# A mixture-of-experts decoder layer on one core: more result buffers, expert blocks added without an order among themselves, two small tables moved, and the last norm on VectorE alone

## The chip, the cores and the metric

The kernel runs on one core of one Trainium2 chip. The metric is the time of one execution in microseconds (us), as the device counts it. Five engines work beside each other, each through its own instructions in its own order: TensorE (PE: matrix products; PEld is its loading of weights), VectorE (DVE), ScalarE (ACT), GpSimd (POOL) and SyncE (SP, which here only issues DMA transfers). An engine that meets an instruction whose input is not there waits, and everything behind it on that engine waits with it.

## The reference

A decoder layer on 1024 tokens of width 1024 in float32: a mixer (gated linear attention and a diagonal state-space model side by side), then a feed-forward part with 32 experts, of which every token uses four, each part between RMS norms and with a modulation from a vector c. The change touches the expert part and the last norm. Cut to them:

```python
logits = (xt @ router_w + router_b)
top_val, top_idx = lax.top_k(logits, TOP_K)         # 4 experts of 32 for each token
gate = jax.nn.softmax(top_val, axis=-1)
...
def expert_block(args):                             # a block of up to 128 tokens of one expert
    xblk, e = args
    gu = xblk @ w_gu[e] + b_gu[e]                   # 1024 -> 2 x 1024
    g, up = gu[:, :D_FF], gu[:, D_FF:]
    g = jnp.minimum(g, SWIGLU_LIMIT)
    up = jnp.clip(up, -SWIGLU_LIMIT, SWIGLU_LIMIT)
    act = (up + 1.0) * (g * jax.nn.sigmoid(SWIGLU_ALPHA * g))
    return act @ w_down[e] + b_down[e]              # 1024 -> 1024
...
out = zeros.at[tok_buf].add(yb * w_buf[:, None])    # every token sums its four weighted results
...
h = h + g2 * rmsnorm(ff, ffn_post_g)                # the last norm
```

## The kernel before

**Stages.** The mixer, the router and the sorting of the tokens by expert take the first 600 us or so. Then comes the expert phase, from about 613 to 1959 us, and behind it a short tail with the last norm. The 32 experts stand in eight groups of four. Each group has a gate-and-up phase (32 chunks of weights) and a down phase (16 chunks); a chunk is 512 x 512 float32 weights, 1 MB, and there are 384.

**A chunk.** SP loads it into one of six stages. ACT makes its float16 high part (L1585), DVE the float16 rest, the low part (L1588, one `scalar_tensor_tensor` of 128 x 2048 with a sum into a column of `gacc` that tells overflow at the end). PE multiplies the high part with both halves of the tokens (L1791, L1792) and the low part with the tokens' high half (L1800).

**Tokens in.** Per block of up to 128 tokens, POOL gathers the rows from `hn_d` by an indirect DMA (L1726), PE transposes them (L1736), and ACT and DVE write them out in two halves.

**Results out.** This is what the change is about. When the four result columns of a half (512 of 1024 columns) of an expert are there, each block of it goes through `out_jobs` (from L1750): PE transposes it into one of two PSUM banks `ot_` (L1759, tile `ax`); ACT (shown at L1602) or DVE (at L143) copies it, times the token's gate weight, into one of three SBUF buffers `yt_r` (tile `A`); POOL issues an indirect DMA that adds the rows to `ff_d[c]` in DRAM (L1765), one tensor for each half c. This is called a scatter below. There are 51 blocks, so 102 scatters. A copy waits until the scatter that last used its buffer has landed. A scatter waits until the scatter before it into the same half has landed, since a token can stand in two experts' lists.

**What sets the order.** In the expert phase every piece of work is a `Job` with the engines that may do it, a duration per engine, a due number, the jobs that it waits for and a `lag` after its end. `run_jobs` goes through them once, when the kernel is built: it gives the engine that is free first the job that is ready first, by the planner's figures, and writes the instruction. So the planner's figures and the waits between jobs set each engine's order, and the chip then keeps to it.

**The tables.** `overflow_table` (L1478 to L1507) builds, out of the counts of tokens per expert, the list of blocks that did not fit; it runs twice, right ahead of the expert phase, some 17 small DVE instructions and three PE products each.

**The last norm** (L1982 to L1997) reads `ff_d` back as eight tiles of 128 tokens, squares and sums each on ACT, multiplies it by a factor GF, and adds it, times a reciprocal root, to the residual; then the tiles go out. It does so in groups of tiles 0-1, 2-5 and 6-7; the multiplications for tiles 0 and 4 are on DVE, the six others on POOL.

## Time and profile before

| what | value |
|---|---|
| median of 3 runs | 2023.61 us (2021.28 to 2032.09) |
| profiled execution | 2024.69 us, its span in the trace 2022.9 us |
| PE busy | 1806.0 us, 89% of the span |
| DVE busy | 1544.2 us, 76% |
| ACT busy | 1199.1 us, 59% |
| POOL busy | 526.5 us, 26% |
| mean granted TensorE clock | 0.948 of full |
| moved by DMA | 540.82 MB, mean 267 GB/s |

The span is the stretch of the trace from the first to the last thing recorded; the time is the device's own, 1.8 us longer. A share of busy time is a mean over stages: PE is at 95% in the expert phase and far lower ahead of it and behind it. In the rows below an engine's line number is that of a helper for many DVE and ACT instructions (L133 is a multiplication, L143 and L145 are operations with a scalar, L148 is `scalar_tensor_tensor`), so the tile names tell what an instruction is. Names left of the arrow are written, names right of it read. [...]

### The profile page before, as it was taken

Reading aid. Unit: us, or ns where it says so; the run is one execution under the profiler, and the core shown is the slowest. Engines: PE = TensorE matmul, PEld = TensorE weight load, DVE = VectorE, ACT = ScalarE, POOL = GpSimd, SP = SyncE. Lnnn points to the kernel's source line nnn. Section 1 sums busy time; section 2 is a strip of 40 time slices with the busy share of each in tenths; the row PEclk is TensorE's granted clock in tenths of the full one; section 3 lists DMA queues with packets and bytes.
Section 4 is the critical chain, followed back from the end, with each engine's and each line's share of the span. In section 5 each row is a group of like instructions: output and inputs, shape, how many; then the busy total and the mean of one; then the engine's idle time right before and its main releaser. Section 6 shows DMA issues by size and latency. Waiting matters only on the chain. (4 is left out here: it accounts for less than half of the span.)

```text
span 2022.9 us, 53263 instructions
## 1 busy us (share of the span) xinstructions
PE 1806.0 (89%) x22354; PEld 1614.5 (80%) x22354; DVE 1544.2 (76%) x2396; ACT 1199.1 (59%) x1682; POOL 526.5 (26%) x495
## 2 busy tenths in 40 slices
PE   8678699998968999998998899999899889999970
PEld 3566588787858999998998899767799789999870
DVE  5766537568767997995997799689799868869835
ACT  3524133544226876875776677577688667768641
POOL 4720012203543025015104402400330330160043
PEclk8889899999978999999999899999999989999985
DMA  9176465323359999999999899888999999999874
GB/s 310 39 193 132 137 196 161 126 70 131 115 172 326 363 322 353 379 351 307 323 329 358 278 351 341 279 323 301 299 367 365 301 296 330 327 318 350 306 192 175
DMA packets 296804, 540.82 MB, mean 267 GB/s; under 512 B 41234, under 2 KB 66032, under 8 KB 296528
## 3 DMA queue, kind: packets, MB, share of 16 engines
q1 hardware_dynamic: 259504, 469.51, 67.5%
q0 software_dynamic: 30384, 60.49, 11.8%
q10 hardware_dynamic: 6672, 7.38, 1.1%
q8 instruction: 177, 2.90, 0.6%
q14 instruction: 67, 0.55, 0.1%
HBM read 489.57 MB, written 45.61 MB: 265 GB/s over the span
## 5 line engine op out<-in xcount | busy, mean ns | idle before, releaser
L1765 POOL DMA_INDIRECT ff_d<-A,S x102 | 260.7, 2555 | 353.8 <-DVE A L143 141.2
L1588 DVE SCALAR_TENSOR_TENSOR B<-A,B 128x2048 f16<-128x2048 f32 x110 | 249.5, 2285 | 33.1 <-ACT B L1585 21.0
L1588 DVE SCALAR_TENSOR_TENSOR E<-A,E 128x2048 f16<-128x2048 f32 x110 | 249.7, 2285 | 16.0 <-ACT E L1585 15.8
L1726 POOL DMA_INDIRECT S<-hn_d,S x51 | 77.8, 1526 | 702.2 <-PE tr L1736 661.7
L1588 DVE SCALAR_TENSOR_TENSOR C<-A,C 128x2048 f16<-128x2048 f32 x110 | 249.7, 2284 | 8.3 <-ACT C L1585 8.2
L1585 ACT ACTIVATE B<-A 128x2048 f16<-128x2048 f32 x110 | 209.2, 1917 | 46.7 <-DMA A<-in_exp_w_gu_dram 36.7
L1585 ACT ACTIVATE E<-A 128x2048 f16<-128x2048 f32 x110 | 208.9, 1917 | 33.1 <-DMA A<-in_exp_w_gu_dram 18.4
L1585 ACT ACTIVATE C<-A 128x2048 f16<-128x2048 f32 x110 | 208.7, 1920 | 25.9 <-PE ax L1792 15.3
L1791 PE MATMUL mm<-S,E 128*128 128x92 f16 (+29 forms) x1336 | 187.8, 230 | 0.6 <-issue 0.5
L1791 PE MATMUL mm<-S,B 128*128 128x164 f16 (+28 forms) x1364 | 185.3, 227 | 3.3 <-issue 3.2
L1792 PE MATMUL mm<-S,B 128*128 128x164 f16 (+28 forms) x1364 | 184.9, 227 | 3.8 <-issue 3.8
L1792 PE MATMUL mm<-S,E 128*128 128x92 f16 (+29 forms) x1336 | 187.5, 229 | 0.0
L1792 PE MATMUL mm<-S,C 128*128 128x92 f16 (+28 forms) x1352 | 183.0, 226 | 3.2 <-issue 3.0
L1791 PE MATMUL mm<-S,C 128*128 128x92 f16 (+28 forms) x1352 | 183.2, 227 | 1.7 <-ACT S L1602 1.7
L1791 PEld LDWEIGHTS <-B 128*128 128x128 f16 x1760 | 154.3, 98 | 16.8 <-issue 9.4
L1791 PEld LDWEIGHTS <-C 128*128 128x128 f16 x1760 | 153.3, 98 | 13.0 <-issue 6.3
L1791 PEld LDWEIGHTS <-E 128*128 128x128 f16 x1760 | 155.0, 98 | 9.6 <-issue 2.0
L1792 PEld LDWEIGHTS <-B 128*128 128x128 f16 x1760 | 154.2, 98 | 9.4 <-issue 2.1
L1792 PEld LDWEIGHTS <-E 128*128 128x128 f16 x1760 | 154.9, 98 | 7.9 <-issue 0.4
L1792 PEld LDWEIGHTS <-C 128*128 128x128 f16 x1760 | 153.0, 98 | 8.3 <-issue 1.8
L148 DVE SCALAR_TENSOR_TENSOR S<-S 128x1 f32<-128x1 f32 (+7 forms) x249 | 106.0, 434 | 42.2 <-DMA S<-in_ada_w_dram 28.4
L1588 DVE SCALAR_TENSOR_TENSOR A<-A,A 128x2048 f16<-128x2048 f32 x54 | 123.5, 2286 | 3.1 <-ACT A L1585 2.9
(353 smaller groups left out, 4266.7 us busy)
## 6 DMA issues: line engine op xcount, KB each, us to landing
A<-in_exp_w_gu_dram SPq DMA_DIRECT2D x256, 1024.0 KB
A<-in_exp_w_down_dram SPq DMA_DIRECT2D x128, 1024.0 KB
S<-in_ada_w_dram POOLq DMA_DIRECT2D x64, 256.0 KB
S<-in_ada_w_dram SPq DMA_DIRECT2D x16, 512.0 KB
S<-in_w_in_dram SPq DMA_DIRECT2D x8, 1024.0 KB
S<-in_x_dram SPq DMA_DIRECT2D x12, 512.0 KB
ff_d<-S POOLq DMA_DIRECT2D x18, 256.0 KB
S<-in_w_out_dram SPq DMA_DIRECT2D x8, 512.0 KB
```

The lines of the kernel that those rows point to most:

```text
L148: V.scalar_tensor_tensor(o, a, s, b, op0=op0, op1=op1, **kw)
L1585: A.activation(WH[n % NWS], ST[n % NST], AF.Copy, scale=WS)
L1588: V.scalar_tensor_tensor(WL[n % NWS], ST[n % NST], WS, WH[n % NWS], op0=OP.mult, op1=OP.subtract, accum_out=acc_col())
L1726: lambda e: P.indirect_dma_start(out=x_[0:cb], out_offset=None, in_=hn2_d, in_offset=bass.IndirectOffsetOnAxis(ap=x.lt[0:cb, b, 0:1], axis ...
L1765: lambda e: P.indirect_dma_start(out=ff_d[c], out_offset=bass.IndirectOffsetOnAxis(ap=x.lt[0:cb, b, 0:1], axis=0), in_=yt[0:cb], in_offset ...
L1791: PE.matmul(pp[q], w_, mh[:, f_], start=(f_ == 0 and q % per == 0), stop=False, skip_group_check=True)
L1792: PE.matmul(pp[q], w_, ml[:, f_], start=False, stop=False, skip_group_check=True)
```

## The change

It does four things.

First, `yt_r` has seven buffers in place of three: four in the tile `A` and three in the tile `S`, behind the token buffers. The room comes from `gacc`, which has 256 columns in another tile in place of 500, and is summed into its first column when it is full.

Second, the scatters of one expert into one half do not wait for each other any more: each waits for `was`, the last scatter of the expert before into that half, and for its own copy. Ahead of each scatter POOL writes a small `spacer` (128 x 1). The planner's figures for a scatter go from 1.7 to 1.9 us on POOL and from 7 to 10 us of lag.

Third, the two overflow tables are planned as jobs at the start of the second group's gate-and-up phase; they use one of the buffers `u_t` and the transposes' PSUM banks.

Fourth, the last norm takes tiles 0-3 and 4-7, and DVE does all eight multiplications.

Loads, the weights' splits and the products stay what they are. Since the planner has other figures, some copies change between ACT and DVE, and some places in the orders move.

```diff
--- before.py
+++ after.py
@@ -1476,7 +1476,7 @@
     ov, nb, starts, jf_, om, ent = small(32), small(32), small(32), small(1), small(32), small(2)
 
     def overflow_table(i, cap):
-        nbt = view(63, 32, 8)
+        nbt = u_t[:, 0:256].rearrange("p (r b) -> p r b", b=8)
         if cap is None:
             V.tensor_copy(ov, cr[:, 0:32])
         else:
@@ -1500,10 +1500,11 @@
         V.tensor_reduce(jf_, om, axis=AX.X, op=OP.add)
         mul(ent[:, 1:2], ent[:, 1:2], jf_)
         yield
-        pe3 = trb(130)
+        pe3 = tr_[i].rearrange("p a b -> p (a b)")[:, 0:130]
         for q in range(2):
             PE.matmul(pe3[0:1, 64 * q:64 * q + 64], ent[0:64, q:q + 1], ident[0:64, 0:64], start=True, stop=True)
         PE.matmul(pe3[0:1, 128:129], jf_, ones[:, 0:1], start=True, stop=True)
+        yield
         V.tensor_copy(otf[0:1, i, 0:129], pe3[0:1, 0:129])
 
     e2, e3 = slot("E2"), slot("E3")
@@ -1519,14 +1520,15 @@
         WL.append(carve(t_, 4, 4, 256).bitcast(F16))
     NST, NWS = len(ST), len(WH)
     a7 = slot("A7")
-    yt_r = [carve(a7, 2 * i, 512) for i in range(3)]
-    gacc = carve(a7, 6, 500)
+    gacc = carve(e3, 7, 256)
     V.memset(gacc, 0.0)
     gs_r, u_t = [carve(e2, 0, 1024), carve(e2, 4, 1024)], carve(e3, 0, 1024)
     CG = max(sum(CAPS[r] for r in g) for g in GROUPS)
     XKB = CG * 32 / 1024
     X0, A0, Y0, XG0 = 0, XKB, 2 * XKB, 2 * XKB + 2 * CAPS[0] / 64
-    assert XG0 + 12 <= 64, XG0
+    YT0 = XG0 + 12
+    yt_r = [carve(a7, 2 * i, 512) for i in range(4)] + [view(YT0 + 2 * i, 512) for i in range(3)]
+    assert YT0 + 6 <= 68.5, YT0
     xg_r = Ring([XG0, XG0 + 4, XG0 + 8], 1024)
     n_acc = [0]
     NBS = [(c_ + 127) // 128 for c_ in CAPS]
@@ -1534,8 +1536,11 @@
     RS = 1.0 / (WS * XS)
 
     def acc_col():
+        if n_acc[0] == 255:
+            V.tensor_reduce(gacc[:, 0:1], gacc, axis=AX.X, op=OP.add)
+            n_acc[0] = 0
         n_acc[0] += 1
-        return gacc[:, n_acc[0] - 1:n_acc[0]]
+        return gacc[:, n_acc[0]:n_acc[0] + 1]
 
     class Expert:
         pass
@@ -1748,7 +1753,7 @@
 
     ot_free, yt_free, added, n_ot = [None] * 2, [None] * len(yt_r), [None] * 2, [0]
 
-    def out_jobs(x, c, b, yT, due, after):
+    def out_jobs(x, c, b, yT, due, after, was, prev):
         cb = min(128, x.C - 128 * b)
         q, y = n_ot[0] % 2, n_ot[0] % len(yt_r)
         n_ot[0] += 1
@@ -1761,10 +1766,14 @@
         ot_free[q] = Job({"ACT": act_us(512, True), "DVE": dve_us(512)}, due + 2, [t_, yt_free[y]],
                          lambda e: scaled(e, yt[0:cb], pt[0:cb].rearrange("p a b -> p (a b)"),
                                           x.lt[0:cb, b, 1:2].bitcast(F32)))
-        yt_free[y] = added[c] = Job({"POOL": 1.7}, due, [ot_free[q], added[c]],
-                                    lambda e: P.indirect_dma_start(
-                                        out=ff_d[c], out_offset=bass.IndirectOffsetOnAxis(ap=x.lt[0:cb, b, 0:1], axis=0),
-                                        in_=yt[0:cb], in_offset=None, compute_op=OP.add), lag=7.0)
+        def put(e):
+            P.memset(spacer, 0.0)
+            a_ = P.indirect_dma_start(out=ff_d[c], out_offset=bass.IndirectOffsetOnAxis(ap=x.lt[0:cb, b, 0:1], axis=0),
+                                      in_=yt[0:cb], in_offset=None, compute_op=OP.add)
+            for o_ in prev:
+                tc.declare_no_dep(a_.ins, o_.ins, reason="each token is in an expert's list once")
+            prev.append(a_)
+        yt_free[y] = added[c] = Job({"POOL": 1.9}, due, [ot_free[q], was], put, lag=10.0)
         return t_
 
 
@@ -1852,7 +1861,8 @@
             ev = Job({"ACT": act_us(nj * C, True, nj), "DVE": dve_us(nj * C, nj)}, due, [end] + wait, results)
             evs.append(ev)
             if js[-1] == 3:
-                place[2].extend(out_jobs(x, c, b, yT, due + 2, list(evs)) for b in range(x.NB))
+                was, prev = added[c], []
+                place[2].extend(out_jobs(x, c, b, yT, due + 2, list(evs), was, prev) for b in range(x.NB))
                 y_used.append(place)
         for q in bi:
             bank_free[q] = ev
@@ -1862,8 +1872,6 @@
     load_list(ex[GROUPS[0][0]])
     biases()
     tables = [overflow_table(0, capr), overflow_table(1, None)]
-    for t_ in tables:
-        take(t_, 2)
     tr_ += [trb(4, 128) for _ in range(2)]
     flat = [(ex[r], b) for r in GROUPS[0] for b in range(NBS[r])]
     for n in range(2):
@@ -1884,6 +1892,11 @@
                 token_jobs(x, b, 2 * i + (span_ - 4) * k / len(todo), [ld[phase[i_ph - 1][0]], step[0]])
         if i_ph < len(phase) and phase[i_ph][1] <= i:
             i_ph += 1
+        if i == phase[2][1]:
+            for q, t_ in enumerate(tables):
+                u_free[0] = Job({"DVE": 4.0}, 2 * i, [u_free[0]] + ([p_] if q else []), lambda e, t_=t_: take(t_))
+                p_ = Job({"PE": 1.0}, 2 * i, [u_free[0], tr_free[q]], lambda e, t_=t_: take(t_))
+                tr_free[q] = Job({"DVE": 0.3}, 2 * i, [p_], lambda e, t_=t_: take(t_))
         sub_jobs(i, *u)
     while made < len(chunks) + 5:
         chunk_jobs(made)
@@ -1982,11 +1995,11 @@
     ss, rr = carve(WT[5], 0, 8), carve(WT[5], 1, 8)
     tv, th = carve(WT[5], 2, 8), carve(WT[5], 3, 8)
     gt = [view(32 + 8 * i, 2, 1024) for i in range(4)]
-    for b_, e_ in ((0,2),(2,6),(6,8)):
+    for b_, e_ in ((0, 4), (4, 8)):
         some = slice(b_, e_)
         for n in range(b_, e_):
             A.activation(jf, ft[n // 2][:, n % 2], AF.Square, scale=RD, accum_out=ss[:, n:n + 1])
-            mul(gt[n // 2][:, n % 2], ft[n // 2][:, n % 2], GF, P if n in (1,2,3,5,6,7) else V)
+            mul(gt[n // 2][:, n % 2], ft[n // 2][:, n % 2], GF)
         ts(ss[:, some], ss[:, some], EPS, OP.add)
         rsqrt(rr[:, some], ss[:, some], tv[:, some], th[:, some])
         for n in range(b_, e_):
```

**Three places in the orders.** The first is ACT near the end of group 5's down phase, at about 1600 to 1625 us in the trace of before. `A_4732<-ax` (and, after, `S<-ax` with 512 columns) is a copy of results into a buffer, `S<-mm` the four result columns of an expert with so many tokens, L1585 (after: L1590) a high part. Before:

```order
L1602 ACTIVATE A_4732<-ax,S 128x512 [waits DMASW6_49,Activation_49]
L1585 ACTIVATE C_4575<-A_4726 128x2048 [waits DMAHW7_49,DVE_49,PE_49]
L1602 ACTIVATE A_4732<-ax,S 60x512 [waits DMASW3_49,DMASW7_49,DVE_49,PE_49]
L1602 ACTIVATE S<-mm,E_4724 128x148 [waits PE_49]
L1602 ACTIVATE S<-mm,E_4724 128x148 x2
L1602 ACTIVATE S<-ax,E_4724 128x148 [waits PE_49]
L1585 ACTIVATE C_4576<-A_4727 128x2048 [waits DMAHW0_49,DVE_49]
L1585 ACTIVATE E_4577<-A_4728 128x2048 [waits DMAHW1_49,DVE_49,PE_49]
L1602 ACTIVATE A_4732<-ax,S 4x512 [waits DMASW2_49]
L1602 ACTIVATE S<-mm,E_4724 128x112 [waits DVE_49,PE_49]
L1602 ACTIVATE S<-mm,E_4724 128x112 x3
L1602 ACTIVATE A_4732<-ax,S 60x512 [waits DMASW3_49,PE_49,Activation_49]
```

After (L1607 is what was L1602):

```order
L1607 ACTIVATE S<-ax,E_4724 128x60 [waits PE_49]
L1607 ACTIVATE S<-ax,E_4724 128x60 x3
L1607 ACTIVATE S<-ax,S 128x512 [waits DMASW6_49,PE_49]
L1607 ACTIVATE S<-ax,S 128x512 [waits DMASW5_49,DMASW7_49,DVE_49,PE_49]
L1590 ACTIVATE E_4578<-A_4728 128x2048 [waits DMAHW7_49,Activation_49]
L1607 ACTIVATE S<-ax,S 4x512 [waits DMASW0_49,PE_49]
L1590 ACTIVATE A_4731<-A_4729 128x2048 [waits DMAHW0_49,Activation_49]
L1607 ACTIVATE S<-mm,E_4724 128x148 [waits PE_49]
L1607 ACTIVATE S<-mm,E_4724 128x148 x2
L1607 ACTIVATE S<-mm,E_4724 128x148 [waits PE_49]
L1607 ACTIVATE A_4732<-ax,S 60x512 [waits DMASW1_49,PE_49]
```

Before, the last copy of the expert of 260 tokens (4 x 512, its third block of the second half) stands behind the result columns of the expert of 148 tokens and behind two more high parts, and waits for a scatter (DMASW2). Now it stands ahead of those result columns, with two copies of 128 tokens next to it that go to buffers in `S`, and the copy waits for DMASW0, the scatter seven copies back.

The second is POOL at the end of the expert phase; `ff_d_748` and `ff_d_749` are the two halves. The DMASW numbers are the queues' counters: where a row names one, it waits for an earlier indirect DMA. Before:

```order
L1765 DMA ff_d_748<-A_4732,S 1152x512 [waits DMASW7_49,Activation_49]
L1765 DMA ff_d_749<-A_4732,S 1152x512 [waits DMASW0_49,DVE_49]
L1765 DMA ff_d_748<-A_4732,S 1152x512 [waits DMASW1_49,DVE_49]
L1765 DMA ff_d_749<-A_4732,S 1152x512 [waits DMASW2_49,Activation_49]
L1765 DMA ff_d_748<-A_4732,S 1152x512 [waits DMASW3_49]
L1765 DMA ff_d_749<-A_4732,S 1152x512 [waits DMASW4_49,Activation_49]
L1765 DMA ff_d_748<-A_4732,S 1152x512 [waits DMASW5_49,Activation_49]
L1765 DMA ff_d_749<-A_4732,S 1152x512 [waits DMASW6_49]
```

After:

```order
L1771 DMA ff_d_748<-S 1152x512 [waits DMASW1_49,DVE_49]
L1770 MEMSET S 128x1 [waits Pool_49]
L1771 DMA ff_d_748<-S 1152x512 [waits DVE_49]
L1770 MEMSET S 128x1 [waits Pool_49]
L1771 DMA ff_d_749<-A_4732,S 1152x512 [waits DMASW5_49,DMASW2_49,DVE_49]
L1770 MEMSET S 128x1 [waits Pool_49]
L1771 DMA ff_d_749<-A_4732,S 1152x512 [waits DVE_49]
L1770 MEMSET S 128x1 [waits Pool_49]
L1771 DMA ff_d_748<-A_4732,S 1152x512 [waits DMASW7_49,DMASW4_49,Activation_49]
L1770 MEMSET S 128x1 [waits Pool_49]
L1771 DMA ff_d_749<-A_4732,S 1152x512 [waits DMASW6_49,DVE_49]
```

Before, halves come in turn. Now the two blocks of an expert in a half come one behind the other, and the second of them has no DMASW wait any more, only that for its copy.

The third is the last norm. On DVE, before, from the second result of the first group on:

```order
L148 SCALAR_TENSOR_TENSOR S<-S,E_4578,A_4725 128x1024 [waits DVE_49]
L148 SCALAR_TENSOR_TENSOR S<-S,E_4578,A_4725 128x1024 [waits Pool_49]
L133 TENSOR_TENSOR S<-S,A_4729 128x1024 [waits DMAHW1_49,DMAHW0_49]
L143 TENSOR_SCALAR E_4578<-E_4578 128x4 [waits Activation_49]
L145 TENSOR_SCALAR E_4578<-E_4578 128x4 [waits DVE_49]
L133 TENSOR_TENSOR E_4578<-E_4578 128x4 [waits DVE_49] x2
L148 SCALAR_TENSOR_TENSOR E_4578<-E_4578 128x4 [waits DVE_49] x2
L133 TENSOR_TENSOR E_4578<-E_4578 128x4 [waits DVE_49] x2
L148 SCALAR_TENSOR_TENSOR E_4578<-E_4578 128x4 [waits DVE_49]
L148 SCALAR_TENSOR_TENSOR S<-S,E_4578,A_4726 128x1024 [waits DVE_49,Pool_49]
L148 SCALAR_TENSOR_TENSOR S<-S,E_4578,A_4726 128x1024 [waits Pool_49]
```

and on POOL, before, the six multiplications:

```order
L133 TENSOR_TENSOR S<-S,A_4729 128x1024 [waits DMAHW5_49,DMAHW4_49]
L133 TENSOR_TENSOR S<-S,A_4729 128x1024 [waits DMAHW7_49,DMAHW6_49]
L133 TENSOR_TENSOR S<-S,A_4729 128x1024
L133 TENSOR_TENSOR S<-S,A_4729 128x1024 [waits DMAHW1_49,DMAHW0_49]
L133 TENSOR_TENSOR S<-S,A_4729 128x1024 [waits DMAHW3_49,DMAHW2_49]
L133 TENSOR_TENSOR S<-S,A_4729 128x1024
```

After, on DVE, the first of the two groups and the start of its results:

```order
L133 TENSOR_TENSOR S<-S,A_4729 128x1024 [waits DMAHW5_49,DMAHW4_49]
L133 TENSOR_TENSOR S<-S,A_4729 128x1024
L133 TENSOR_TENSOR S<-S,A_4729 128x1024 [waits DMAHW7_49,DMAHW6_49]
L133 TENSOR_TENSOR S<-S,A_4729 128x1024
L143 TENSOR_SCALAR E_4578<-E_4578 128x4 [waits Activation_49]
L145 TENSOR_SCALAR E_4578<-E_4578 128x4 [waits DVE_49]
L133 TENSOR_TENSOR E_4578<-E_4578 128x4 [waits DVE_49] x2
L148 SCALAR_TENSOR_TENSOR E_4578<-E_4578 128x4 [waits DVE_49] x2
L133 TENSOR_TENSOR E_4578<-E_4578 128x4 [waits DVE_49] x2
L148 SCALAR_TENSOR_TENSOR E_4578<-E_4578 128x4 [waits DVE_49]
L148 SCALAR_TENSOR_TENSOR S<-S,E_4578,A_4725 128x1024 [waits DVE_49]
L148 SCALAR_TENSOR_TENSOR S<-S,E_4578,A_4725 128x1024
```

The six rows on POOL are gone; DVE has two multiplications per pair of tiles, each pair behind its reads (DMAHW), and one short chain of 128 x 4 instructions per group, two chains where there were three.

## Rows read from the trace of the kernel before

**Rows 1.** Page, part 1, TensorE: busy time, share of the span, instructions.
```profile
PE 1806.0 (89%) x22354; PEld 1614.5 (80%) x22354; DVE 1544.2 (76%) x2396; ACT 1199.1 (59%) x1682; POOL 526.5 (26%) x495
```

**Rows 2.** Stretches: length, busy PE, PEld, DVE, ACT, POOL, clock, DMA share, GB/s.
```profile
613.00:1959.00 1346.00, 1283.83 (x19218) 1196.75 (x19219) 1125.16 (x1415) 952.41 (x1164) 315.35 (x143) 0.98 0.97 326
820.00:880.00 60.00, 60.00 (x990) 59.99 (x988) 57.74 (x62) 49.81 (x66) 0.24 (x1) 1.00 1.04 379
1480.00:1510.00 30.00, 30.00 (x560) 29.50 (x556) 29.65 (x38) 26.32 (x36) 12.65 (x5) 1.00 1.04 369
760.00:800.00 40.00, 38.15 (x573) 37.30 (x572) 29.43 (x35) 25.43 (x30) 22.53 (x11) 1.00 1.05 352
```

**Rows 3.** Waits from 640 to 1945: engine, line, what for, us, times, longest.
```profile
ACT A L1602 <- DMA ff_d<-A,S: 81.1, 19, 13.0
DVE A L143 <- DMA ff_d<-A,S: 26.8, 9, 8.1
PE ax L1759 <- DVE A L143: 18.5, 7, 6.1
PE ax L1759 <- ACT A L1602: 15.7, 3, 12.4
```

**Rows 4.** Timeline, 1605 to 1626: start, us, engine, line; in brackets the idle before.
```profile
1606.32 2.02 POOL L1765 DMA_INDIRECT ff_d<-A,S  x1 [0.30 <-issue]
...
1622.15 0.68 ACT L1602 ACTIVATE A<-ax,S 4x512 f32<-4x512 f32 x1 [8.16 <-DMA ff_d<-A,S]
...
1622.88 1.06 PE L1759 MATMUL ax<-S 128*60 128x128 f32 x4 [12.40 <-ACT A L1602]
1622.94 1.48 POOL L1765 DMA_INDIRECT ff_d<-A,S  x1 [9.61 <-ACT A L1602]
```

**Rows 5.** Five stretches behind such waits, columns as in Rows 2, and their sum.
```profile
943.10:946.50 3.40, 3.40 (x18) 2.29 (x16) 3.40 (x3) 0.00 (x0) 3.40 (x1) 0.50 0.48 105
...
sum 20.00, PE 17.39 PEld 15.95 DVE 14.04 ACT 7.34 POOL 13.58; mean PE 3.48 PEld 3.19 DVE 2.81 ACT 1.47 POOL 2.72
```

**Rows 6.** Page, part 5, the group of the scatters.
```profile
L1765 POOL DMA_INDIRECT ff_d<-A,S x102 | 260.7, 2555 | 353.8 <-DVE A L143 141.2
```

**Rows 7.** Timeline, 1790 to 1792: the longest issue, the first split beside it.
```profile
1790.77 15.05 POOL L1765 DMA_INDIRECT ff_d<-A,S  x1 [3.44 <-DVE B L1588]
1791.03 2.27 DVE L1588 SCALAR_TENSOR_TENSOR C<-A,C 128x2048 f16<-128x2048 f32 x1
```

**Rows 8.** Timeline, 525 to 526: a scatter behind a small memset, on GpSimd.
```profile
525.40 0.96 POOL L1409 DMA_INDIRECT L_d<-S  x1 [0.18 <-issue]
```

**Rows 9.** Timeline, 597 to 604: ends of the two tables, and ACT beside them.
```profile
597.96 0.28 DVE L1507 COPY S<-tr 1x129 f32<-1x129 f32 x1 [0.58 <-PE tr L1506]
...
600.38 1.91 ACT L1585 ACTIVATE B<-A 128x2048 f16<-128x2048 f32 x1 [6.92 <-DMA A<-in_exp_w_gu_dram]
...
602.24 0.28 DVE L1507 COPY S<-tr 1x129 f32<-1x129 f32 x1 [0.58 <-PE tr L1506]
```

**Rows 10.** Timeline, 1971 to 1992: last scatters, and the read behind them.
```profile
1971.86 1.59 POOL L1765 DMA_INDIRECT ff_d<-A,S  x1 [2.38 <-ACT A L1602]
...
1977.43 1.40 POOL L1765 DMA_INDIRECT ff_d<-A,S  x1 [1.29 <-DMA ff_d<-A,S]
...
1983.66 2.14 SPq L1980 DMA_DIRECT2D S<-ff_d  x4
```

**Rows 11.** Timeline, 1985 to 2023: the final norm on GpSimd and VectorE.
```profile
1993.03 11.57 POOL L133 TENSOR_TENSOR S<-S,A 128x1024 f32<-128x1024 f32 x5 [0.70 <-DMA S<-ff_d]
...
1995.43 4.59 DVE L133 TENSOR_TENSOR E<-E 128x2 f32<-128x2 f32 x2
...
2006.81 1.21 DVE L133 TENSOR_TENSOR S<-S,A 128x1024 f32<-128x1024 f32 x1
...
2009.80 4.87 DVE L148 SCALAR_TENSOR_TENSOR S<-S,E,A 128x1024 f32<-128x1024 f32 x4
...
2016.44 2.48 DVE L148 SCALAR_TENSOR_TENSOR S<-S,E,A 128x1024 f32<-128x1024 f32 x2
```

## The prediction

> **What bounds the kernel now.** I read the page's first part first: TensorE is busy 89% of the span [rows 1], so time can come only from where it idles, or runs at the lower clock. The view by stretches says where. In the expert phase, 613 to 1959 us, PE is busy 1283.83 of 1346 us, so 62 us are idle, at a mean clock of 0.98; from 820 to 880 it is busy all the time at the full clock while 379 GB/s come in [rows 2]. So the weights can keep PE busy, and something else opens the gaps.
>
> The view of waits names it. ACT's and DVE's copies of results into `yt_r` wait 81.1 + 26.8 = 107.9 us for scatters [rows 3]. Those engines have room. But PE's transposes (L1759), which need one of two PSUM banks back from such a copy, sit idle 18.5 + 15.7 = 34.2 us in ten waits [rows 3], and the products behind them in PE's order with them. The timeline shows one whole: a scatter is issued at 1606.32, the copy of 4 x 512 waits for one until 1622.15, PE's next transposes start at 1622.88 after 12.40 us of nothing, and the next scatter follows at 1622.94 [rows 4]. It is a ring: three buffers, a scatter that may not start before its forerunner has landed, and a landing that takes many us under load.
>
> [...]
>
> The time behind the expert phase is a chain too. After the products end, at about 1959, the last scatters go out one landing apart, the last at 1977.43; the read behind the overflow loop starts at 1983.66 [rows 10]. In the last norm POOL multiplies 11.57 us long, and DVE's tiny steps beside it take 4.59 us for two where four whole tiles take 4.87 [rows 11].
>
> **The change part by part.** Durations are from the profiled execution, so the sum is made against its 2024.69 us (span 2022.9 and 1.8 around it); the median of the runs is 1.08 less.
>
> *Buffers and unordered additions: -37.8 us.* They go together, since either alone leaves a chain: seven buffers with ordered scatters still drain at a landing each, unordered scatters with three buffers still wait for the third back. With both, a copy waits for the scatter seven back, which is seven issues of 2.56 us [rows 6] or 18 us earlier when POOL issues without a pause; from the issue at 1606.32 to the copy at 1622.15 are 15.8 us [rows 4]. So a landing of that length just fits, and the mean one well. I take the 34.2 us of PE's idle time as gone, and with it the half clock: 17.39 us of work at half clock would take half, so 8.6 us more. What is late next? Two of the ten waits, I guess, stay: a copy on DVE can stand behind a split of 2.27 us [rows 7] whatever the ring does, and weights have that much less lead. 2 x 2.5 = 5 us off: 34.2 + 8.6 - 5 = 37.8. The other 28 us of idle time in the phase have other causes (the first expert, weights late) and stay. Bounds: nothing returns below (0, if the ring merely fills later), 42.8 above.
>
> DVE gets some 10 of ACT's copies, at about 0.7 us each (one on ACT takes 0.68 [rows 4]), 7 us more. It is busy 1125.16 of 1346 us [rows 2], so it would be at about 88% of the shorter phase with the tables' 8.6 us: still below PE. From 1480 to 1510 it is at 29.65 of 30 while PE does not idle [rows 2], so even there it keeps up.
>
> *The spacer memsets: 0.* 102 more instructions on POOL. At 525.40 an indirect DMA behind a memset begins 0.18 us after it [rows 8], and the memset is 0.11 long; two scatters without one begin 0.30 after each other already (the gap at 1606.32 [rows 4]). So it fits in the gap. At worst it is 102 x 0.29 = 30 us on POOL, which idles beside PE for three quarters of the phase (315.35 of 1346 busy [rows 2]): 0 on the path. POOL's queue holds the gathers of the next group behind scatters; by order the number of both is as before.
>
> *Tables: 0.* The copies that end them stand at 597.96 and 602.24 [rows 9], so one takes 4.3 us and both 8.6 us of DVE ahead of the phase; now they stand at the second group's start. From 760 to 800 DVE is busy 29.43 of 40 [rows 2], so 10.6 us are free there and hide them; bare, they cost up to 8.6. Ahead of the phase I expect nothing back: ACT's high part at 600.38 had waited 6.92 us for its weights, not for the tables, and ends as the tables do [rows 9]. Seven gathers that start earlier may meet the first loads. I allow 2 us less and 3 more, and take 0.
>
> *The end of the scatters: -8.6 us.* Products are through at about 1959, the first copies 2 us later. Before, the last scatter is issued by 1977.43 + 1.40 = 1978.8 [rows 10]. Now the two blocks of one expert in a half go one behind the other. The second half's two go at about 1961.3 and 1963.2, the latter issued by 1964.8; the last expert's block waits for that one's landing. In this quiet stretch the landing takes 4.0 us: the scatter of 1971.86 is issued by 1973.45, and the one at 1977.43 waits for it [rows 10]. So 1968.8, and 1.4 more for its issue: 1970.2, 8.6 earlier. Bounds: 4 (one more landing in the chain) and 11.
>
> *The last norm: -5.3 us.* Tiles 2 and 3 are read at 1993.03 [rows 11]; two multiplications of 1.21 end at 1995.45; the short chain takes 1.78 (2006.81 + 1.21 = 2008.02 to 2009.80); four results 4.87; four multiplications 4.84; chain 1.78; four results 4.87: 2013.59, against 2016.44 + 2.48 = 2018.92. Bounds: 3, if the reads end later, and 6.
> The short chain before, stretched while POOL multiplies (two instructions of 128 x 2 in 4.59 us, where the whole later chain takes 1.78), is part of what goes. [...]
>
> Sum: 37.8 + 8.6 + 5.3 = 51.7. 2024.69 - 51.7 = 1973.0; less 1.08 for the median, **1972 us**.
>
> **The rivals.**
>
> *A: half of the stalls come back.* POOL's issue is slow while DVE splits without a pause: the one at 1790.77 lasts 15.05 us, as long as six splits [rows 7]. If the mean issue in the down phases rose to 3.5 us, seven would take 25 us, and with a landing behind them the ring would fill again at the experts of three and four blocks, which have six or eight scatters in a row. Against it: the mean over all 102 is 2.56 [rows 6], and from 1480 to 1510, DVE 99% busy, five POOL instructions take 12.65 together [rows 2]. Half of 37.8 back: 1972 + 19 = 1991.
> [...]
>
> *B: the weights become the bound.* 326 GB/s in 1346 us would have to be 336 in 1306; 379 were there for 60 us with PE at 100% [rows 2]. So it is unlikely. If the rate went only half that way, to 331, the phase would be 326 x 1346 / 331 = 1326, a gain of 20 in place of 38: 1990.
>
> *C: the change does not do what it says,* because the waits stay by dependences between tiles. Only the norm's 5.3 and half of the tail's 8.6 then come: 2024 - 10 = 2014. The order after shows second blocks without a wait on a DMA, so I hold it small.
>
> *D: slower than before, POOL's queue as the bound.* The gathers for the next group stand behind the scatters in POOL's order. A down phase of 16 chunks at 1346/384 = 3.5 us is 56 us. POOL's 143 instructions in the phase take 315.35 us [rows 2], 2.2 each; 18 of them a group take 40. So the 13 scatters of a group may grow by 16/13 = 1.2 us each, to 3.8, before POOL sets the pace. From there each further us costs 13 us a group, 91 over seven, and the gain of 51.7 is used up at 4.4 us. If unordered scatters, each now free to start while others are still adding to memory, took 5.0 us to issue, the time were 1972 + 1.2 x 91 = 2081. The mean is 2.56 [rows 6]: unlikely.
>
> **How the numbers follow.** Forecast (a gain of 38 to 65 us): 0.70, with its own range 1958 to 1986. A 0.15, B 0.06, C 0.06, D 0.03. Within half a per cent, about 10 us, is what a measurement of this kernel cannot tell from no change. Faster by more than that: the forecast, A, B and half of C, 0.94; same: the other half of C, 0.03; slower: D, 0.03. The range reaches down to 1953 for what the planner's other order may close of the remaining idle 28 us, and up over A and B to 1996; C and D lie outside.
>
> **What would show it.** In the profile after: PE's idle time at the results' transposes under 10 us; the copies' waits for scatters under 30; PE busy over 0.97 of the expert phase at a clock of 0.98 or more; last scatter some 10 us behind PE's last product; one DVE run of about 20 us from the second pair's reads to the end. Wrong would be: a mean issue on POOL above 3.5 us, gathers late for PE's transposes (L1736), or new idle time of PE behind low parts on DVE.

## The result, and the profile after

The changed kernel takes 1973.32 us (median of four runs, 1972.01 to 1974.39); before took 2022.44 in its four. The ratio is 0.9754, with a 95% interval from 0.9712 to 0.9797: faster by 2.5%. The forecast was 1972. The profiled execution takes 1974.39 us, span 1972.6, so 50.3 us less than that of before. In the two traces they lie here (the first tile is read when the first of its multiplications starts):

| stretch | before | after | change | forecast |
|---|---|---|---|---|
| start to first expert product | 613.7 | 610.5 | -3.2 | 0 |
| first to last expert product | 1345.3 | 1307.5 | -37.8 | -37.8 |
| last product to last scatter | 18.4 | 13.5 | -4.9 | -8.6 |
| last scatter to first tile read | 11.5 | 11.5 | 0 | 0 |
| first tile read to the end | 34.0 | 29.6 | -4.4 | -5.3 |

The -3.2 at the start is no part of the change that can be told: over the versions run below the first product lay between 609.1 and 618.0 us.

TensorE's line on the page of the kernel after, against [rows 1], and the expert phase from its first to its last product, columns as in [rows 2]:

```profile
PE 1796.7 (91%) x22354; PEld 1609.7 (82%) x22354; DVE 1543.9 (78%) x2407; ACT 1195.2 (61%) x1669; POOL 505.8 (26%) x591
```

```profile
610.50:1918.00 1307.50, 1275.21 (x19227) 1190.31 (x19226) 1135.61 (x1456) 952.25 (x1156) 312.69 (x237) 0.99 0.99 336
```

PE is busy 1275.21 us for the same products that took 1283.83 [rows 2], and idle 32.3 us in place of 62.2. So about 8 us are busy time, at a mean granted clock of 0.99 of full speed for 0.98, and 30 are idle time. The 336 GB/s is what the prediction said would be asked for, and it was there.

The view of waits of the kernel after, 640 to 1945 us, against [rows 3]:

```profile
POOL ff_d L1771 <- DMA ff_d<-A,S: 40.1, 11, 9.7
...
DVE S L143 <- PE ax L1764: 18.0, 5, 9.1
...
PE ax L1764 <- ACT S L1607: 1.3, 1, 1.3
...
PE ax L1764 <- DVE A L143: 0.5, 1, 0.5
...
PE ax L1764 <- ACT A L1607: 0.3, 1, 0.3
```

No copy waits for a scatter any more: the two rows of 81.1 and 26.8 us are gone, and copies wait for PE instead. PE's idle time at the results' transposes (now L1764) is 2.1 us in the three rows that name a copy, where it was 34.2. Scatters still wait for scatters, 40.1 us in the row above and 5.9 in another, but until the products end no other engine is named as waiting for one; behind the last product two such waits count, as the tail below shows.

The timeline of the kernel after at the place of [rows 4], a copy of 4 tokens and the transposes of 60 in group 5:

```profile
1565.37 0.66 ACT L1607 ACTIVATE S<-ax,S 4x512 f32<-4x512 f32 x1
...
1568.01 0.60 PE L1764 MATMUL ax<-S 128*60 128x128 f32 x4
```

There is no bracket on the copy or on the transposes: the 12.40 us and the 8.16 us of [rows 4] are not there. The two groups of scatters on the page of the kernel after (from `A` and from `S`: busy us, mean ns of one); then the group from `A` once more with its least, middle and longest issue in ns; then the least, middle and longest time from an issue to its landing, of the 40 scatters whose landing the trace holds:

```profile
L1771 POOL DMA_INDIRECT ff_d<-A,S x60 | 152.2, 2537 | 74.8 <-ACT A L1607 22.4
...
L1771 POOL DMA_INDIRECT ff_d<-S x42 | 89.1, 2122 | 187.7 <-DVE S L143 126.9
...
L1771 POOL DMA_INDIRECT ff_d<-A,S x60: 1364/1946/8547, 743.7 to 1931.5; - x60
...
DMA to landing us min/median/max: 4.3/9.1/17.6
```

Over all 102 an issue takes 2.37 us in the mean, no more than before (2555 ns in [rows 6]). A landing takes 9.1 us in the middle and up to 17.6.

The tail after, against [rows 10]:

```profile
1918.66 1.57 POOL L1771 DMA_INDIRECT ff_d<-S  x1 [1.72 <-DMA ff_d<-A,S]
...
1922.50 1.57 POOL L1771 DMA_INDIRECT ff_d<-A,S  x1 [0.22 <-issue]
...
1924.37 1.61 POOL L1771 DMA_INDIRECT ff_d<-A,S  x1 [0.19 <-DMA ff_d<-S]
...
1926.68 1.42 POOL L1771 DMA_INDIRECT ff_d<-A,S  x1 [0.58 <-issue]
...
1931.55 1.43 POOL L1771 DMA_INDIRECT ff_d<-A,S  x1 [3.33 <-DMA ff_d<-A,S]
...
1937.94 2.31 SPq L1993 DMA_DIRECT2D S<-ff_d  x4
```

The last norm after, on DVE, against [rows 11]:

```profile
1943.01 2.36 DVE L133 TENSOR_TENSOR S<-S,A 128x1024 f32<-128x1024 f32 x2 [19.66 <-DMA S<-ff_d]
...
1947.68 2.36 DVE L133 TENSOR_TENSOR S<-S,A 128x1024 f32<-128x1024 f32 x2 [2.31 <-DMA S<-ff_d]
...
1951.88 4.87 DVE L148 SCALAR_TENSOR_TENSOR S<-S,E,A 128x1024 f32<-128x1024 f32 x4
...
1962.98 4.87 DVE L148 SCALAR_TENSOR_TENSOR S<-S,E,A 128x1024 f32<-128x1024 f32 x4
```

The multiplications are pairs of 2.36, the four results 4.87 as in [rows 11], and nothing stretches the chain between them: its pairs of multiplications of 128 x 4 take 0.36 us (at 1950.50), where the pair of 128 x 2 beside POOL's multiplications took 4.59 [rows 11].

### The profile page after: what moved, and what is told of

Same layout as the page of the kernel before. It is cut to its first block, busy times and chain, and to the rows that moved or that the text cites. A ratio compares the mean times of both kernels' runs of the same rounds, so it can differ in the third digit from the quotient of the medians.

```text
span 1972.6 us, 53347 instructions
## 1 busy us (share of the span) xinstructions
PE 1796.7 (91%) x22354; PEld 1609.7 (82%) x22354; DVE 1543.9 (78%) x2407; ACT 1195.2 (61%) x1669; POOL 505.8 (26%) x591
## 5 line engine op out<-in xcount | busy, mean ns | idle before, releaser
L1593 DVE SCALAR_TENSOR_TENSOR E<-A,E 128x2048 f16<-128x2048 f32 x110 | 249.7, 2286 | 17.6 <-ACT E L1590 17.6
L1590 ACT ACTIVATE B<-A 128x2048 f16<-128x2048 f32 x110 | 209.3, 1919 | 69.0 <-DMA A<-in_exp_w_gu_dram 52.9
L1590 ACT ACTIVATE C<-A 128x2048 f16<-128x2048 f32 x110 | 209.5, 1919 | 45.2 <-DMA A<-in_exp_w_gu_dram 24.7
L1590 ACT ACTIVATE E<-A 128x2048 f16<-128x2048 f32 x110 | 209.1, 1916 | 41.8 <-DMA A<-in_exp_w_gu_dram 24.9
L1771 POOL DMA_INDIRECT ff_d<-A,S x60 | 152.2, 2537 | 74.8 <-ACT A L1607 22.4
L1771 POOL DMA_INDIRECT ff_d<-S x42 | 89.1, 2122 | 187.7 <-DVE S L143 126.9
```

The lines of the kernel that those rows point to most:

```text
L1590: A.activation(WH[n % NWS], ST[n % NST], AF.Copy, scale=WS)
L1593: V.scalar_tensor_tensor(WL[n % NWS], ST[n % NST], WS, WH[n % NWS], op0=OP.mult, op1=OP.subtract, accum_out=acc_col())
L1771: a_ = P.indirect_dma_start(out=ff_d[c], out_offset=bass.IndirectOffsetOnAxis(ap=x.lt[0:cb, b, 0:1], axis=0), in_=yt[0:cb], in_offset=None ...
```

## The experiments

All are edits of the changed kernel and were timed against the kernel before. "Phase" is the time from the first to the last expert product in the profiled execution.

**Neither buffers nor unordered scatters (ordered3).**

```diff
-yt_r = [... for i in range(4)] + [view(YT0 + 2 * i, 512) for i in range(3)]
+yt_r = [carve(a7, 2 * i, 512) for i in range(3)]
-            for o_ in prev:
-                tc.declare_no_dep(a_.ins, o_.ins, ...)
-            prev.append(a_)
-Job({"POOL": 1.9}, due, [ot_free[q], was], put, lag=10.0)
+Job({"POOL": 1.9}, due, [ot_free[q], added[c]], put, lag=10.0)
```

> The changed kernel with neither of its first two parts: three buffers, and scatters in one order within a half; tables, norm, spacer and the planner's new figures stay. My theory: the 37.8 us of the expert phase come from these two alone, so the phase is back at about 1345 us, the scatters' tail at 18 us behind the last product; only the norm's 4.4 us stay of the gain: 2015 to 2020. Rival: the planner's new figures (1.9 and 10 us) move the transposes so that part of the waits is gone without the buffers: under 2005.

Measured: 1998.87 us, ratio 0.9887 [0.9852, 0.9921]; phase 1323.3, in the fastest of its four executions (1995.32). The rival's number came out; whether for its reason is open, as said below. Without either of the two parts 22 of the phase's 37.8 us are already there; the last scatter comes 17.4 us behind the last product, as forecast. Its waits, 640 to 1945:

```profile
POOL ff_d L1771 <- DMA ff_d<-A,S: 87.9, 23, 10.1
...
PE ax L1764 <- ACT A L1607: 20.2, 11, 3.7
...
ACT A L1607 <- DMA ff_d<-A,S: 16.2, 9, 3.2
...
DVE A L143 <- DMA ff_d<-A,S: 8.1, 6, 4.6
...
POOL ff_d L1771 <- ACT A L1607: 97.1, 20, 12.2
```

Two rows of the kernel before, same stretch:

```profile
POOL ff_d L1765 <- DMA ff_d<-A,S: 76.9, 19, 8.5
...
POOL ff_d L1765 <- ACT A L1602: 36.9, 12, 9.6
```

Copies wait 24 us for scatters, not 108 [rows 3], though the ring is as short and the scatters as ordered as before. The 84 us did not turn into waits of scatters for scatters (87.9 us against 76.9). What grew is POOL's wait for copies on ACT, 97.1 us against 36.9: the copies come later. PE's 20.2 us at the transposes hold 7.3 behind the last product; in the phase it is 12.9 in this row. Counted in the two traces, 40 of the 102 transposes of results stand later in PE's order than before, by up to 352 products, and none earlier. That fits the planner's longer figure for a landing (10 us in place of 7; the middle landing in the changed kernel takes 9.1): it no longer puts a transpose where its buffer is not yet back. That it is this figure, and not the tables' new place or the 1.9 us for an issue, was not run apart. In the changed kernel itself it goes the other way: 25 of the 102 stand earlier than before, by up to 376 products, and none later.

**Buffers alone (ordered7).** The last two edits of the diff above, without the first: seven buffers, ordered scatters.

```diff
-            for o_ in prev:
-                tc.declare_no_dep(a_.ins, o_.ins, ...)
-            prev.append(a_)
-Job({"POOL": 1.9}, due, [ot_free[q], was], put, lag=10.0)
+Job({"POOL": 1.9}, due, [ot_free[q], added[c]], put, lag=10.0)
```

> The changed kernel, but with the scatters in one order again: each waits for the scatter before it into the same half. Seven buffers stay, and the spacer memsets. My theory (the prediction's): the ring alone is not enough, since ordered scatters drain at one landing each in a half, so that the buffers fill in the down phases; at least half of the 37.8 us of the expert phase comes back and the 5 us of the tail: 1998 us or more, with copies waiting for scatters again for over 40 us. Rival one: seven buffers alone do it, since a down phase's backlog of scatters is drained in the next gate phase; then only the tail's 5 us come back: about 1978, copies' waits under 10 us.

Measured: 1990.26 us, ratio 0.983 [0.9784, 0.9876]; phase 1316.7, last scatter 18.8 us behind the last product. Between the two: a quarter of the phase's gain is lost, and the tail's 5 us.

```profile
POOL ff_d L1771 <- DMA ff_d<-A,S: 83.1, 20, 11.7
...
PE ax L1764 <- ACT A L1607: 12.6, 1, 12.6
```

One wait of 12.6 us is most of it, at 1604.6, where group 5's last results are transposed between group 6's first products. But no row of this view has a copy wait for a scatter, which was a sign of rival one: the scatters wait in POOL's queue, and the ring of seven holds them. The copy that PE waits for stands on ACT behind high parts, of which the first had waited for its weights:

```profile
1595.15 1.91 ACT L1590 ACTIVATE E<-A 128x2048 f16<-128x2048 f32 x1 [6.64 <-DMA A<-in_exp_w_gu_dram]
...
1603.87 0.66 ACT L1607 ACTIVATE A<-ax,S 20x512 f32<-20x512 f32 x1
```

In PE's order six of the 102 transposes stand later than in the changed kernel, by up to 176 products. That this other order makes the wait was not tried.

**Unordered scatters alone (free3).**

```diff
-yt_r = [... for i in range(4)] + [view(YT0 + 2 * i, 512) for i in range(3)]
+yt_r = [carve(a7, 2 * i, 512) for i in range(3)]
```

> The changed kernel, but with three buffers as before; the scatters of an expert in a half stay unordered. My theory: with three buffers a copy still waits for the scatter three back, a landing of about 9 us for three blocks; at least half of the 37.8 us comes back: 1992 us or more, PE idle over 15 us at the transposes of results. Rival two: taking the order away alone does it, since then three scatters are under way at once, some 4 us for each, about what a down phase asks for: 1980 us or less.

Measured: 1995.15 us, ratio 0.9855 [0.9811, 0.9898]; phase 1328.2. My theory held.

```profile
ACT A L1607 <- DMA ff_d<-A,S: 30.6, 9, 8.1
...
DVE A L143 <- DMA ff_d<-A,S: 27.2, 6, 7.2
...
PE ax L1764 <- ACT A L1607: 20.6, 11, 6.0
...
PE ax L1764 <- DVE A L143: 4.7, 2, 3.2
```

Copies wait 57.8 us again, PE 25.3 at the transposes, 3.7 of it behind the last product. Against neither part (1998.87) taking away the order alone gives 3.7 us and seven buffers alone 8.6, by medians from two sets of runs; both intervals overlap that of ordered3. In the phase taking away the order alone gives nothing (1328.2 against 1323.3). Both together give 27 (1971.39 in the same set of runs as ordered3).

**Four buffers, unordered (free4).**

```diff
-yt_r = [... for i in range(4)] + [view(YT0 + 2 * i, 512) for i in range(3)]
+yt_r = [carve(a7, 2 * i, 512) for i in range(4)]
```

> The changed kernel, but with four buffers, those that lie in the old tile; none in the token tile. My theory: between three and seven, about a quarter of the 37.8 us comes back: about 1983. Rival two (the order alone counts): 1973 to 1976, no different from seven.

Measured: 1972.88 us, ratio 0.9759 [0.9704, 0.9815]; phase 1307.3. It is no different from seven, as the rival had it, but not for the rival's reason: free3 shows that the order alone does not do it.

```profile
ACT A L1607 <- DMA ff_d<-A,S: 21.5, 9, 9.4
...
DVE A L143 <- DMA ff_d<-A,S: 6.9, 3, 4.3
...
PE ax L1764 <- ACT A L1607: 5.9, 4, 2.0
```

Copies wait 28 us for scatters, but PE only 7.4 for copies (5.9 in the row shown, 1.5 in one for DVE). With unordered scatters all the gain of the ring lies between three buffers and four; the three in the token tile give nothing that could be measured.

**Planner's old figures (lag7).**

```diff
-Job({"POOL": 1.9}, due, [ot_free[q], was], put, lag=10.0)
+Job({"POOL": 1.7}, due, [ot_free[q], was], put, lag=7.0)
```

> The changed kernel with the planner's old figures for a scatter (1.7 us on GpSimd, 7 us of lag). My theory: with buffers to spare the order hardly hangs on them: 1971 to 1976. Rival: the planner then puts scatters and copies too early and waits return: over 1980.

Measured: 1971.65 us, ratio 0.9729 [0.9702, 0.9756]; phase 1307.1. My theory held. In PE's order not one of the 102 transposes stands elsewhere than in the changed kernel.

**Tables ahead of the phase (tables_start).**

```diff
+    for t_ in tables:
+        take(t_, 3)
...
-        if i == phase[2][1]:
-            for q, t_ in enumerate(tables):
-                ...
```

> The changed kernel, but with both overflow tables built ahead of the expert phase again, as before the change. My theory: in the second group they are hidden, and ahead of the phase they take back the 3.2 us by which the phase now starts earlier, of which group 0's gate phase keeps only about 1: so 1973 to 1975, no difference that can be told. Rival: the start counts in full, 1976 to 1977. Other rival: the tables are bare in the second group and cost up to 8.6 us there, so without them it is 1965 to 1968.

Measured: 1970.67 us (1964.84 to 1973.91), ratio 0.9731 [0.9684, 0.9777]. It lies between my theory and the second rival and is not told from the changed kernel. In the profile the first product comes at 615.3, 4.8 us later, and the last at 1915.3, 2.8 earlier, so the phase is 7.6 us shorter. The start itself is no proof: the first product moved between 609.1 and 618.0 also where nothing ahead of it was changed. Of the transposes in PE's order none stands elsewhere than in the changed kernel.

**The old last norm (old_norm).**

```diff
-    for b_, e_ in ((0, 4), (4, 8)):
+    for b_, e_ in ((0,2),(2,6),(6,8)):
-            mul(gt[n // 2][:, n % 2], ft[n // 2][:, n % 2], GF)
+            mul(gt[n // 2][:, n % 2], ft[n // 2][:, n % 2], GF, P if n in (1,2,3,5,6,7) else V)
```

> The changed kernel with the last norm as before the change: groups of two, four and two tiles, six of eight multiplications on GpSimd. My theory: the 4.4 us between the two profiles (34.0 against 29.6 us from the first tile's landing to the span's end) are the norm's alone: 1977 to 1979, and DVE's small instructions stretched again while GpSimd multiplies. Rival: the reads set the pace there and the norm gives nothing: 1972 to 1975.

Measured: 1973.96 us (1971.32 to 1977.78), ratio 0.9755 [0.9715, 0.9796]. The time alone would say that the norm gives nothing. The profile says otherwise: from the first tile's read to the end it is 34.0 us again, as before, against 29.6. This execution's last product came 3 us sooner (1915.0 against 1918.1) and its last scatter 3.7, which hid it; the three other executions were not traced. DVE and POOL in the old norm:

```profile
1939.31 1.22 DVE L133 TENSOR_TENSOR S<-S,A 128x1024 f32<-128x1024 f32 x1 [18.98 <-DMA S<-ff_d]
...
1943.40 11.59 POOL L133 TENSOR_TENSOR S<-S,A 128x1024 f32<-128x1024 f32 x5 [0.67 <-DMA S<-ff_d]
...
1945.84 4.58 DVE L133 TENSOR_TENSOR E<-E 128x2 f32<-128x2 f32 x2
...
1965.37 0.36 DVE L133 TENSOR_TENSOR E<-E 128x2 f32<-128x2 f32 x2
```

Two instructions of 128 x 2 take 4.58 us beside GpSimd's multiplications, as in [rows 11], and 0.36 us in the last group, when GpSimd is through. The edit also brings back the groups of two, four and two tiles; what each of the two gives was not run apart.

**Dearer scatters (slow3, slow6).**

```diff
             P.memset(spacer, 0.0)
+            for _ in range(3):                       # 6 in slow6
+                P.memset(view(YT0 + 6, 400), 0.0)
```

> The changed kernel with three more memsets, of 128 x 400, on GpSimd ahead of every scatter, some 0.5 us each by my estimate, so about 1.5 us more per scatter. The prediction's rival D puts the point from which GpSimd sets the pace at 3.8 us for an issue; 2.54 + 1.5 = 4.0 is just above: 0.2 x 91 = 18 us, 1992. Rival: the point lies far higher, since a down phase's scatters may run over into the next gate phase as long as the gathers keep their lead; then 1973 to 1977.

> The same with six memsets, about 3 us more per scatter. By the prediction's rival D: 2.54 + 3.0 = 5.5 us, 1.7 above the point, 1.7 x 91 = 155 us, so about 2130. By the other view (GpSimd is busy 313 of 1308 us, so there is room for 9 us a scatter over the whole phase): the ring of seven fills at the large experts, 10 to 30 us: 1983 to 2003.

Measured: slow3 1974.53 us, ratio 0.9768 [0.9727, 0.9808]; slow6 2006.68 us, ratio 0.9921 [0.99, 0.9942]. Busy time in the phase, slow3 and then slow6, columns as in [rows 2]:

```profile
612.00:1914.00 1302.00, 1270.60 (x19229) 1186.40 (x19228) 1135.83 (x1456) 952.27 (x1157) 449.69 (x528) 0.99 0.99 337
```

```profile
609.00:1936.00 1327.00, 1277.72 (x19216) 1192.21 (x19215) 1138.18 (x1456) 953.48 (x1156) 577.98 (x811) 0.99 0.98 331
```

POOL's busy time goes from 313 to 450 and 578 us, so 1.3 and 2.6 us more per scatter; the 1.5 and 3 expected were an estimate of mine, from no run shown. The first costs nothing that the time shows; in its profile the phase is no longer (1301.8), and the last scatter comes 17.1 us behind the last product in place of 13.5. The second costs 33 us; in its profile the phase has 20 of them (1327.3) and the tail 15, where each scatter now stands 4.7 us behind the last, in place of 1.9:

```profile
1960.63 1.42 POOL L1773 DMA_INDIRECT ff_d<-A,S  x1 [0.37 <-issue]
...
1965.32 1.42 POOL L1773 DMA_INDIRECT ff_d<-A,S  x1 [0.34 <-issue]
```

By the prediction's formula slow6 would have been 155 us later by the estimate, or 106 by the measured 2.6 (2.37 + 2.6 = 5.0 us an issue, 1.16 above 3.8, times 91). Nor is its cause in the phase the one of rival D, gathers that come late. Rows of slow6's waits, 640 to 1945:

```profile
DVE A L143 <- DMA ff_d<-A,S: 22.2, 4, 11.7
...
ACT S L1607 <- DMA ff_d<-S: 7.1, 2, 4.4
...
PE tr L1741 <- DVE S L148: 0.7, 1, 0.7
```

PE hardly idles at the transposes of tokens, which need the gathers (L1741, 0.7 us). The copies wait for scatters again, 36.8 us with two smaller rows, where the changed kernel has none: the ring of seven fills, as the other view had it. PE stands little at the copies themselves (1.4 us) but elsewhere, for instance where a waiting copy on DVE holds up a split:

```profile
1437.74 0.75 DVE L143 TENSOR_SCALAR S<-ax,S 88x512 f32<-88x512 f32 x1 [6.33 <-DMA ff_d<-S]
...
1440.76 1.05 PE L1811 MATMUL mm<-S,C 128*128 128x260 f16 x4 [4.87 <-DVE C L1593]
```

How much of the 20 us comes this way is not shown.

**Another order in the last group (tail).**

```diff
-          [4, 29, 7, 22], [3, 26, 5, 31]]
+          [4, 29, 7, 22], [3, 26, 31, 5]]
```

> The changed kernel with the last group's experts in another order: 252, 68, 36 and 228 tokens in place of 252, 68, 228 and 36. The last scatter now waits for the landing of the scatters of the 228-token expert just ahead of it (3.33 us idle on GpSimd, and its own landing behind). With that expert last its two blocks wait only for the 36-token expert's scatter, issued some 10 us earlier. My theory: the last scatter comes about 7 us after TensorE's last product in place of 13.5, so 1966 to 1968. Rival: the larger expert's own copies at the end take as long, or the planner's order loses elsewhere: 1972 to 1976.

Measured: 1972.21 us (1966.02 to 1975.7), ratio 0.9737 [0.9696, 0.9777]. In the profile the last scatter comes 8.9 us behind the last product in place of 13.5, without a wait; but the read of `ff_d` starts 8.9 us after it, where it was 6.4:

```profile
1930.54 1.59 POOL L1771 DMA_INDIRECT ff_d<-A,S  x1 [0.19 <-issue]
...
1939.47 2.25 SPq L1993 DMA_DIRECT2D S<-ff_d  x4
```

So half of the 4.6 us is given back. The last four scatters go out one behind the other, 1.9 us apart (from 1924.90 to 1930.54); whether they land together is not shown, and what the read waits for is not named. The whole is not told from no change.

**The three single edits together (best4), beside the changed kernel once more (after_again).** Four buffers, tables ahead of the phase, the last group's new order; the edits are those shown above.

```diff
+yt_r = [carve(a7, 2 * i, 512) for i in range(4)]
...
+    for t_ in tables:
+        take(t_, 3)
...
+          [4, 29, 7, 22], [3, 26, 31, 5]]
```

> The changed kernel with four buffers in place of seven, both tables ahead of the expert phase, and the last group's experts in the order 252, 68, 36, 228 tokens: the three single edits that came out no slower, together. Their medians stood 0.4, 2.7 and 1.1 us under that of the changed kernel. My theory: they add up to about 4 us, 1969. Rival: each was within the scatter of the runs, and together they give nothing: 1971 to 1975.

> The changed kernel once more, unaltered, on the same chip as the version with the three edits, so that the two can be compared: 1970 to 1976.

Measured: best4 1965.16 us (1961.39 to 1969.84), ratio 0.9698 [0.9674, 0.9723]; the changed kernel 1971.39 (1969.11 to 1973.38), ratio 0.973 [0.9708, 0.9752]. So the version with the three edits is the fastest here, some 6 us or 0.3% under the changed kernel; the two intervals still overlap, so the gain is likely rather than shown. The phases of the two, best4 first:

```profile
613.00:1913.00 1300.00, 1270.71 (x19217) 1187.07 (x19217) 1125.03 (x1420) 952.23 (x1159) 316.82 (x241) 0.99 0.99 338
```

```profile
610.60:1917.00 1306.40, 1273.36 (x19230) 1188.78 (x19228) 1135.31 (x1456) 952.22 (x1157) 319.25 (x238) 0.99 0.99 336
```

PE is nearly 4 us less idle in these 1300 us than in 1306.4, and 2.7 us less busy. DVE does 1125 us in place of 1135: the tables are out of the phase.

## Why the prediction came out right

**The sum.** It is off by 1.4 us in the profiles (50.3 against 51.7), and partly by luck: the tail and the norm gave 4.6 us less than forecast, and the start, for which nothing was forecast and which moves by as much between versions, gave 3.2.

**What bounds.** Right. The gaps at PE's results' transposes were the place: 34.2 us of idle time there became 2.1, 0.5 of it behind the last product. PE's busy time fell by about 8 us for the same products, against the 8.6 that were worked out for the half clock: in the five stretches of [rows 5], each at a granted clock of 0.50 or 0.51, PE is 17.39 us busy (halved 8.7). The two waits that I let stand (5 us) did not stay as such: 1.6 us stayed at the transposes and 2.7 us of idle time came up elsewhere, so 37.8 was met partly by luck.

**"They go together, since either alone leaves a chain."** Right in that neither does it alone: by the medians, from the base of ordered3, buffers alone give 8.6 us and taking away the order alone 3.7, neither told from nothing, and both give 27. The chain that was named for buffers alone is not seen: in ordered7 no copy waits for a scatter, and what the order costs there shows as one wait behind high parts on ACT and in the tail. What the prediction missed is that the planner's new order had no term: I said only that the numbers of scatters and gathers are as before, and did not ask what a longer landing in the plan does to the transposes in a short ring. With neither part 22 of the phase's 37.8 us are there already (ordered3). That does not take the gain from the two parts: with both, the planner's old figures give the same time (lag7), so they earn the 37.8 without the new ones. There are two ways to much of the same gain, and they overlap: a later transpose keeps PE from standing at a late buffer, the ring and the unordered scatters make the buffer come early. That the planner's figures are what helps without the two parts is argued from the order, not shown.

**Seven buffers.** "A landing of that length just fits" was the reason for seven. Four do as well (free4), so the fit was no reason.

**Memsets, tables.** They cost nothing, as forecast: even 1.3 us more on POOL for each scatter cost nothing in the phase (slow3). Taking the tables back out of the second group is not told from no change alone. DVE is busy 1135.61 of 1307.5 us, 87%, and the prediction's own terms give 87% too, where it says 88.

**End of the scatters, -8.6.** Mis-sized: -4.9. I had the last two blocks of the second half go out at 2.3 and 4.2 us behind the last product. They went at 4.4 and 6.3 (1922.50 and 1924.37 against 1918.1), because the first half's two stood ahead of them in POOL's queue, and the first of those waited 1.72 us for the expert before. From the end of the second one's issue to the last scatter it was then 5.6 us (1925.98 to 1931.55) in place of the 4.0 of [rows 10].

**The last norm, -5.3.** It is -4.4 by the profile, and old_norm gives that back. On DVE it is as worked out: 24.8 us from the first read to the last result (24.7 in the working). But from the last result's end to the span's end are 4.75 us in place of 3.98; perhaps because the last four results now leave together, which was not tried.

**The rivals.** A did not come: issues took 2.37 us in the mean, at most 8.5, and no copy waited for a scatter. Whether DVE's splits slowed the issue of 15.05 us [rows 7] the runs do not decide. B did not come either: 336 GB/s came in with PE 97.5% busy. Nor did C: ordered3 has waits that the changed kernel has not. D's point was wrong and its mechanism was not seen: at 5.0 us an issue the phase was 20 us longer, not 106, and it was copies that waited for scatters, not PE for gathers.

## What to carry to other kernels

Where an order is planned ahead, a duration in the plan that is shorter than the measured one can show as an in-order engine waiting behind a buffer that the plan thought free; compare the plan's figure with the trace's first, before room is spent on buffers (here 7 us were planned for a landing, and 9.1 measured in the middle in the changed kernel; that the figure matters is argued from ordered3, and with the buffers in place the figure no longer mattered). A ring and an ordering constraint that feed the same wait are tested together, with neither and with each alone, since their gains need not add (here 8.6 and 3.7 us alone, 27 together). A gain of a few us in a tail is read from the profile's stretch, not from the whole time, which here moves by as much between runs (1971.32 to 1977.78 in old_norm).

## What the hardware showed that I had not expected

PE waits at some places of the program in both kernels for nothing that the trace shows, for example ahead of the expert of 36 tokens in group 7, 2.54 us in the kernel before (at 1900.11) and 2.28 us in the one after:

```profile
1861.15 0.18 PE L1800 MATMUL mm<-S,C 128*128 128x36 f16 x1 [2.28 <-issue]
```

From 1861.9 to 1865.3, behind it, the granted clock was 0.50 of full speed: products of 128 x 252 began 0.21 us apart (from 1862.01), 0.11 apart at 1.00 (in the kernel before, from 1846.27). The changed kernel has four such gaps of 2.2 to 2.5 us (1424.2, 1615.0, 1806.2, 1861.2). Not each is followed by the lower clock: in the kernel before, behind one of 2.29 us at 1845.80, the granted clock stays at 1.00 until 1855. What they wait for was not tried. A scatter's landing varied from 4.3 to 17.6 us in one execution, that of the changed kernel.
